# The output projection of a hybrid layer as seven products of half-size blocks instead of eight

## The chip, the cores and the metric

The kernel runs on one core of a Trainium2 chip. The metric is the device time of one execution in microseconds (us), the median of several runs. The engines are named as the profile names them: PE (TensorE, matmuls; PEld are its weight loads), DVE (VectorE), ACT (ScalarE), POOL (GpSimd) and SP (SyncE, which here only issues DMAs).

## What is computed

One layer over 512 tokens of 1024 features: RMSNorm, a combined input projection with 4616 columns, four mLSTM heads and eight heads of block-sparse attention, each with a gate, and one output projection into the residual. All of it is float32. The change touches the end:

```python
def _layer(x, norm_w, w_in, ..., w_out, slopes):
    h = _rmsnorm(x, norm_w)
    proj = h @ w_in
    ...
    y_ml = h_ml.reshape(B, S, ML_WIDTH) * jax.nn.silu(ml_z)      # 512 features
    ...
    y_at = o_at.reshape(B, S, AT_WIDTH) * jax.nn.silu(at_z)      # 512 features
    y = jnp.concatenate([y_ml, y_at], axis=-1) @ w_out           # (512 x 1024) @ (1024 x 1024)
    return x + y
```

## The kernel before

Operands of matmuls are split: a value is kept as a high part in the format fp32r (names ending in hi or h) and the remainder as a low part, fp32r too (lo, l). A product is three matmuls, high by high, high by low and low by high (`mm3`); one of them has 128 x 128 stationary and up to 512 moving columns, and accumulates in a bank of PSUM. A tile is split by two instructions, a cast on ACT that writes the high part and a subtraction on DVE that writes the low one.

The program runs in stages by chunks of w_in's columns: z, aq, ak, av, qk0, qk1, mo, mv and az. Each chunk has 8 k-tiles. Weights come in pieces of two k-tiles, 128 x 1024 elements, 512 KB: SP loads a piece into one of three tiles named raw (`load_w`), ACT casts it to whi, DVE subtracts to wlo (`g_split`); there are six whi and six wlo. az is the last chunk and gives the gate of attention, transposed (features on partitions): `ev_z` multiplies the bank by the tokens' norms on DVE, applies Silu on ACT, multiplies with the attention's result `ot` on DVE, and leaves y_at in cv0 and cv1, four tiles of 128 features by 512 tokens. The mLSTM programs (`g_mlstm`, one for each of four heads) end beside az: PE transposes a head's result into a bank, and `put_y` writes its high part (ACT, with the norm's weight as scale) and its low part (DVE) into two tiles named br. `put_y` does the same for y_at into xh and xl.

The output projection follows. Its k-tiles 0 to 3 are the heads' (br), 4 to 7 attention's (xh, xl). The first half of the output's columns goes tile of 128 tokens by tile, first k 0 to 3 for all four tiles, then k 4 to 7; the second half goes tile after tile with all eight k, and the last tile there is cut into two of 256 columns. All in all that is 4 x 2 x 8 x 3 = 192 matmuls of 512 columns, or their equivalent. Eight pieces of w_out go the way of the weights. x is loaded into tq and tk once they are free; `ev_out` adds a bank and x on DVE, in place, and SP stores the tile.

Everything is one stream per engine, in the order in which the program issues it when it is built. The main stream issues the matmuls; all else are programs (generators) that a planner (`Plan`) resumes between matmuls, when what they wait for is estimated to be there: `Engine` keeps a clock for each engine from costs by element. Nearly all work of DVE, ACT and POOL thus goes through one line of a helper, L75. Matmuls are L173, transposes L177, weight loads L234, loads of x L860, stores L868. On the chip each engine runs its instructions in that order and stops at the first one whose semaphores have not come.

Of the kernel before, what the change touches and what calls it, by code (L numbers as in the profile page):

```python
# [51 lines left out]
class Engine:  # L52
    """Issues to one engine and keeps an estimate of when it gets through."""
# [76 lines left out]

@with_exitstack
def hybrid_layer(ctx: ExitStack, tc: tile.TileContext, xT, x, w_in, w_out, smalls, out):
# [34 lines left out]
    # ---- TensorE  # L167
# [14 lines left out]
    # the table of Silu and the clock of TensorE come up while the first loads run  # L182
# [11 lines left out]
    # ---- weights, in pieces of two k-tiles  # L194
    pieces = []
    off = 0
    for name, cols in _chunks():
        n = len(cols)
        for kk in range(4):
            pieces.append((name, kk, n, w_in, off))  # L200
            off += P * 2 * n
    off = 0
    for half in range(2):
        for kk in range(4):
            pieces.append((f"wo{half}", kk, 512, w_out, off))
            off += P * 2 * 512
# [14 lines left out]
    def load_w(dst=None, between=None):  # L221
        i = nload[0]
        if i >= len(pieces) or (dst is None and i - max(nsplit[0], 5) >= 3):
            return
# [23 lines left out]

    def split_w():
        i = nsplit[0]  # L250
        if i < len(pieces):
            nsplit[0] += 1
            plan.add(g_split(i), rank=1)
# [5 lines left out]
    # ---- constants  # L259
# [12 lines left out]
    # ---- long-lived tiles  # L272
# [19 lines left out]
    xps = Bufs(plan, [sb(f"xp{i}", [P, S + 3]) for i in range(2)])  # L292
    for _, xp in xps.free:
        nc.gpsimd.memset(xp[:, 0:3], 0.0)
# [4 lines left out]
    # ---- startup: x^T and the first weights, into room that is not yet in use  # L299
# [42 lines left out]
    # ---- the three products of the two parts  # L342
# [18 lines left out]

    def group(g, mul, evac):
# [8 lines left out]
    # ---- what follows a projection  # L371
# [53 lines left out]
    # ---- gates of the mLSTM heads  # L425
# [68 lines left out]
    # ---- attention  # L494
# [148 lines left out]
    # ---- mLSTM  # L643
    yh, yl = {}, {}

    def put_y(f, src, scale, t_=0.0):
        hi, lo = (br.get(), br.get()) if f < 4 else (xh[:, f - 4], xl[:, f - 4])
        if scale is None:
            yield act.copy(hi, src)
            t_ = dve.tensor_tensor(lo, src, hi.bitcast(F32), op=ALU.subtract)  # L650
        else:
            yield act.activation(hi, src, AF.Copy, scale=scale)
            t_ = dve.scalar_tensor_tensor(lo, src, scale, hi.bitcast(F32), op0=ALU.mult, op1=ALU.subtract)
        yh[f], yl[f] = hi, lo
        yield t_

    def g_mlstm(h):
# [100 lines left out]
        for t_ in put_y(h, ps, sm[:, C_MN + h:C_MN + h + 1]):  # L758
            yield t_
# [4 lines left out]
    def ev_z(f):  # L764
        z = cv[f // 2][:, f % 2]

        def ev(ps):
# [5 lines left out]
            yield when(lambda: have["proj"], t_)  # L773
            for t_ in put_y(4 + f, z, None):
                yield t_
        return ev

    have["proj"] = 0

    # ---- main stream  # L780
# [62 lines left out]
    plan.until(lambda: have["silu"] == 3)  # L843
    for f in range(4):
        group(f, lambda ps, k: feat_mm(ps, "az", f, k), ev_z(f))
    have["proj"] = 1

    def out_mm(ps, half, t, k, c0=0, c1=512):
        plan.until(lambda: k in yh)
        hi, lo = need_w(f"wo{half}", k // 2)  # L850
        ts = slice(t * P, (t + 1) * P)
        mm3(ps[:, :c1 - c0], yh[k][:, ts], yl[k][:, ts], hi[:, k % 2, c0:c1], lo[:, k % 2, c0:c1],
# [74 lines left out]
```

## Time and profile before

| | us |
|---|---|
| median of 3 runs | 310.79 |
| lowest and highest run | 310.39, 310.81 |
| span of the profiled execution | 308.8 |
| last projection chunk ends, output projection begins on PE | 260.5 |
| last matmul starts | 305.04 |

The profiled execution's own time outside the profiler is not known; its span runs from the first to the last recorded work, and the median of the runs lies 2.0 us above it. In the page, the first part gives each engine's busy time, and the fourth the chain of work that ended last. A window row has the busy time of each engine between two points of the span, then the granted clock of PE as a share of full speed, the share of the DMA engines' time and the rate. A timeline row has the start, the duration from the first instruction's start to the last one's end, the engine, and what it writes from what; "x3" means three alike in a row. Buffer numbers are left out of the names.

### The profile page before, as it was taken

The numbers are of one execution on the slowest core, as the hardware profiler recorded it, in microseconds if no ns is written. First come the engines' busy times: TensorE is split into PE (matmuls) and PEld (weight loads), VectorE is DVE, ScalarE is ACT, GpSimd is POOL, SyncE is SP. The second block draws the span as 40 slices with busy tenths as digits, with TensorE's granted clock in tenths as the row PEclk, the third lists the DMA queues.
The fourth block names the chain that finished last, engine by engine and source line by source line (L and its number), as shares of the span: only waits on it lengthen the run. The fifth ranks groups of instructions, "written<-read, shape, count | busy, mean of one in ns | idle before, by whom it ended". The sixth has DMA issues, their size and how long they took to land.

```text
span 308.8 us, 4284 instructions
## 1 busy us (share of the span) xinstructions
PE 303.2 (98%) x1594; PEld 248.2 (80%) x1594; DVE 185.8 (60%) x395; ACT 150.2 (49%) x271; POOL 58.3 (19%) x94
## 2 busy tenths in 40 slices
PE   7999999999999999999999999999999999999995
PEld 3999888778888868886886888688889978788885
DVE  4892458935456549999627995501568999714111
ACT  3372754314365671775439356899763237420000
POOL 3000164262501800450150005110000060000000
PEclk9999999999999999999999999999999999999999
DMA  7997122141410410132103021400252102832101
GB/s 198 394 412 300 68 69 75 63 137 49 155 70 0 168 39 9 60 128 78 68 2 137 0 83 55 138 0 2 93 176 73 44 24 72 306 135 102 36 34 68
DMA packets 10821, 31.80 MB, mean 103 GB/s; under 512 B 1328, under 2 KB 1584, under 8 KB 10800
## 3 DMA queue, kind: packets, MB, share of 16 engines
q1 hardware_dynamic: 10800, 31.53, 28.8%
q8 instruction: 12, 0.20, 0.3%
q14 instruction: 9, 0.07, 0.1%
HBM read 29.42 MB, written 2.10 MB: 102 GB/s over the span
## 4 chain that ended last, share of the span: by engine, by line
PE 95%; DMA 2%; SPq 1%; DVE 1%; ACT 0%; issue 0%
PE bank L173 89%; PE bank L177 6%; DMA tq<-in_xT_dram 2%; ACT xh L75 0%; DVE wlo L75 0%; SPq L306 0%; DVE xl L75 0%; SPq L234 0%; SPq L232 0%; DVE tk L75 0%; SPq L230 0%; SPq L180 0%
## 5 line engine op out<-in xcount | busy, mean ns | idle before, releaser
L173 PE MATMUL bank<-whi,xh 128*128 128x512 f32 (+2 forms) x260 | 86.4, 367 | 0.7 <-DVE whi L75 0.7
L173 PE MATMUL bank<-wlo,xh 128*128 128x512 f32 (+2 forms) x260 | 85.1, 363 | 0.2 <-DVE wlo L75 0.2
L173 PE MATMUL bank<-whi,xl 128*128 128x512 f32 (+2 forms) x260 | 85.2, 363 | 0.0
L75 DVE TENSOR_TENSOR wlo<-raw,whi 128x1024 fp32r<-128x1024 f32 x39 | 48.0, 1241 | 10.8 <-ACT whi L75 9.2
L173 PEld LDWEIGHTS bank<-whi,xh 128*128 128x128 f32 x260 | 45.1, 188 | 8.7 <-ACT xh L75 1.1
L173 PEld LDWEIGHTS bank<-whi,xl 128*128 128x128 f32 x260 | 45.0, 188 | 8.1
L173 PEld LDWEIGHTS bank<-wlo,xh 128*128 128x128 f32 x260 | 45.1, 188 | 7.9 <-DVE wlo L75 0.6
L75 ACT CAST whi<-raw 128x1024 fp32r<-128x1024 f32 x39 | 40.8, 1048 | 19.8 <-PE bank L173 11.5
L173 PE MATMUL bank<-xh,whi 128*128 128x512 f32 x96 | 40.9, 426 | 0.0
L173 PE MATMUL bank<-xh,wlo 128*128 128x512 f32 x96 | 37.9, 395 | 0.0
L173 PE MATMUL bank<-xl,whi 128*128 128x512 f32 x96 | 37.7, 393 | 0.0
L75 POOL TENSOR_SCALAR b<-b,rec 128x128 f32<-128x128 f32 (+3 forms) x32 | 18.9, 612 | 84.6 <-DVE rec L75 67.1
L75 ACT ACTIVATE br<-bank,sm 64x512 fp32r<-64x512 f32 (+1 forms) x28 | 19.1, 684 | 14.7 <-DVE br L75 9.7
L173 PEld LDWEIGHTS bank<-xh,whi 128*128 128x128 f32 x96 | 18.2, 190 | 4.5 <-issue 2.1
L173 PE MATMUL bank<-whi,br 128*128 128x512 f32 (+1 forms) x72 | 21.4, 370 | 0.0
L173 PEld LDWEIGHTS bank<-xh,wlo 128*128 128x128 f32 x96 | 18.0, 188 | 4.2
L75 ACT ACTIVATE b<-b,mn 128x128 f32<-128x128 f32 (+3 forms) x32 | 17.6, 553 | 7.6 <-DVE mn L75 7.5
L173 PEld LDWEIGHTS bank<-xl,whi 128*128 128x128 f32 x96 | 18.2, 189 | 2.5
L75 DVE SCALAR_TENSOR_TENSOR br<-bank,sm,br 64x512 fp32r<-64x512 f32 (+1 forms) x20 | 15.0, 749 | 5.9 <-ACT br L75 5.6
L75 DVE CUSTOM_DVE_ANT_0 b<-bank,b 128x128 f32<-128x128 f32 (+3 forms) x32 | 14.2, 488 | 5.5 <-PE bank L173 5.4
L173 PEld LDWEIGHTS bank<-whi,br 128*128 128x128 f32 x72 | 13.1, 188 | 2.6
L177 PEld LDWEIGHTS bank<-ident,b 128*128 128x128 f32 (+1 forms) x104 | 12.3, 140 | 3.4 <-issue 0.4
(141 smaller groups left out, 374.1 us busy)
## 6 DMA issues: line engine op xcount, KB each, us to landing
raw<-in_w_in_dram SPq DMA_DIRECT2D x31, 512.0 KB, 3.2
raw<-in_w_out_dram SPq DMA_DIRECT2D x8, 512.0 KB, 3.5
b<-in_w_in_dram SPq DMA_DIRECT2D x3, 520.0 KB, 7.5
tq<-in_xT_dram SPq DMA_DIRECT2D x4, 256.0 KB, 5.4
tk<-in_xT_dram SPq DMA_DIRECT2D x4, 256.0 KB, 7.8
ot<-in_x_dram SPq DMA_DIRECT2D x2, 512.0 KB, 9.1
cv<-in_x_dram SPq DMA_DIRECT2D x2, 512.0 KB, 9.9
tq<-in_x_dram SPq DMA_DIRECT2D x4, 256.0 KB, 5.8
```

The source lines that it names most:

```text
L75: fn(out, *args, **kw)
L173: nc.tensor.matmul(out_, lhsT=lhsT, rhs=rhs, start=start, stop=stop, skip_group_check=True)
L177: nc.tensor.transpose(out_, in_, idn)
```

## The change

With x on the left in halves by tokens (H0, H1) and features (mLSTM, attention) and w_out in four blocks (11, 12, 21, 22), the eight products of blocks become seven, each 256 tokens x 512 features by 512 x 512:

- p5: y_ml of H1 by 11+12; p1: x1 = y_ml H0 - y_at H0, by 11; p2: y_at H0 by 21+11; p6: r = y_ml H1 - x1, by 11-22; p3: c = y_ml H0 - y_ml H1, by 12+22; p7: e = r - y_at H1, by 22; p4: y_at H1 by 21+22. This is also their order on PE.

Each has 4 k-tiles, 2 tiles of 128 tokens and 3 matmuls of 512 columns, 24 in all; the second token tile of p4 is cut into two of 256 columns. Bank pair A accumulates p1, p6, p7 and p4 without a restart, pair B p5 and p3, a third pair p2. What stands in a bank between two products is taken out: after p5, p1 and p6 by a copy on ACT (with scale 1 or -1) into a result tile, to which POOL then issues an accumulating DMA of x from HBM; after p2, p3, p7 and p4 by an addition on DVE into the result tiles. SP stores them.

Sums of weight blocks: 11+12, 21+11, 12+22 and 21+22 are made by a plain load by SP and an accumulating DMA (accum_op add, issued by POOL) of the second block onto it; 11-22 by DVE. Sums of x by DVE, their splits by ACT and DVE. `put_ml` now writes a head's result as float32 to tq on ACT, and splits only H1 at once. The six loads that p5, p1 and p2 need run beside az (`g_load`); the rest of the stage is collected as tasks with costs and set in order by a list scheduler (`Stage`), engine by engine. xp0 and xp1 are one tensor now, since one sum lands there. Lines of the new kernel: matmuls L230, loads L335 and L1041, accumulating loads L339, L1049 (weights) and L1152 (x), casts L1091 and L1110, subtractions L1095, L1105 and L1111, sums for p6 L1085, copies L1151, additions L1141.

```diff
+        if len(AT[tag]) == 2:
+            nc.gpsimd.dma_start(dst, w_src(*AT[tag][1], u), accum_op=ALU.add)
...
-    def put_y(f, src, scale, t_=0.0):
-        hi, lo = (br.get(), br.get()) if f < 4 else (xh[:, f - 4], xl[:, f - 4])
...
-            yield act.activation(hi, src, AF.Copy, scale=scale)
-            t_ = dve.scalar_tensor_tensor(lo, src, scale, hi.bitcast(F32), op0=ALU.mult, op1=ALU.subtract)
...
+    def put_ml(h, ps, scale, t_=0.0):
+        yield act.activation(yml[:, h], ps, AF.Copy, scale=scale)
+        hi, lo = X["p5"]
+        t_ = act.copy(hi(h), yml[:, h, H[1]])
         yield t_
+        yield dve.tensor_tensor(lo(h), yml[:, h, H[1]], hi(h).bitcast(F32), op=ALU.subtract)
...
-    def out_mm(ps, half, t, k, c0=0, c1=512):
...
-    def ev_out(half, t, c0=0, c1=512):
...
+    CHAIN = {"p5": ("B", (1, 1, ADD, False)), "p1": ("A", (0, 0, ADD, False)),
+             "p2": ("1", (0, 0, ADD, True)), "p6": ("A", (0, 1, SUB, False)),
+             "p3": ("B", (0, 1, ADD, True)), "p7": ("A", (1, 1, SUB, True)),
+             "p4": ("A", (1, 0, ADD, True))}
...
+    def load(tag, blk, dst, plus=None, after=()):
+        BT[tag] = dst
+        BL[tag] = st.add("SP", 1450.0, dma(dst, w_src(*blk)), after, lat=2500.0)
+        if plus:
+            BL[tag] = st.add("POOL", 1000.0, lambda: nc.gpsimd.dma_start(dst, w_src(*plus), accum_op=ADD), [BL[tag]], lat=6000.0)
...
+                sums[name, u] = t_ = st.add("DVE", 1240.0, lambda src=src, w2=w2, op=op: nc.vector.tensor_tensor(src, src, w2, op=op), dep)
...
+            dep += (parts(NAMES[n - 3], k=2 * u + 1) if n > 2 else []) + [last]
+            last = st.add("ACT", 1050.0, f_hi, dep)
+            lows[name, u] = t_ = st.add("DVE", 1240.0, f_lo, [last])
...
+        x1.append(st.add("DVE", 420.0, vec(xav[:, f], yml[:, f, H[0]], y_at[f][:, H[0]]), z))
+        xs1.append(split("p1", f, xav[:, f], [x1[f]]))
...
+        if name in ("p5", "p1", "p6"):
+
+            sign = -1.0 if op == SUB else 1.0
+            t_ = st.add("ACT", 640.0, lambda: nc.scalar.activation(d, bank[key, a], AF.Copy, scale=sign), deps)
+            prev[r, c, a, c0] = st.add("POOL", 1000.0, lambda: nc.gpsimd.dma_start(d, x_of(r, c, a), accum_op=ADD), [t_], lat=6000.0)
+            return t_
```

Three places of the order follow. In a row, names carry buffer numbers, and "waits" names the semaphores: Activation, DVE, PE and Pool are engines, DMAHW a DMA that SP issued, DMASW one that POOL issued.

PE at the beginning of the output projection; br are the operands made from mLSTM's results, whi and wlo the weights. Before:

```order
L173 MATMUL bank5_91<-whi_1992,br_0_78 128x512 [waits Activation_49]
L173 MATMUL bank5_91<-wlo_1993,br_0_78 128x512
L173 MATMUL bank5_91<-whi_1992,br_7_85 128x512
L173 MATMUL bank5_91<-whi_1992,br_2_80 128x512 [waits Activation_49]
L173 MATMUL bank5_91<-wlo_1993,br_2_80 128x512
L173 MATMUL bank5_91<-whi_1992,br_3_81 128x512 [waits DVE_49]
```

After, from the same row number:

```order
L230 MATMUL bank1_87<-whi_2062,br_0_78 128x512 [waits Activation_49]
L230 MATMUL bank1_87<-wlo_2063,br_0_78 128x512
L230 MATMUL bank1_87<-whi_2062,br_2_80 128x512 [waits DVE_49]
L230 MATMUL bank4_90<-whi_2062,br_0_78 128x512
L230 MATMUL bank4_90<-wlo_2063,br_0_78 128x512
L230 MATMUL bank4_90<-whi_2062,br_2_80 128x512
L230 MATMUL bank1_87<-whi_2062,br_0_78 128x512 [waits Activation_49]
```

The stage begins at the same place of PE's stream, with two token tiles (two banks) by turns on one weight instead of one token tile after another.

DVE before the projection's first results: the gating of the last head (sz, mst), then lows of br, of weights (wlo) and of x (xl). Before:

```order
L75 SCALAR_TENSOR_TENSOR b5_2_71<-b5_2_71,mst_2213,sz_127 128x128 [waits DVE_49] x2
L75 SCALAR_TENSOR_TENSOR br_3_81<-bank3_89,sm_94,br_2_80 128x512 [waits Activation_49]
L75 TENSOR_TENSOR wlo_2257<-raw_2020,whi_2256 128x1024 [waits DMAHW4_49,PE_49,Activation_49]
L75 TENSOR_TENSOR cv1_132<-cv1_132,ot_133 128x512 [waits Activation_49]
L75 SCALAR_TENSOR_TENSOR br_1_79<-bank2_88,sm_94,br_4_82 128x512 [waits Activation_49]
L75 TENSOR_TENSOR wlo_2280<-raw_2045,whi_2279 128x1024 [waits DMAHW5_49,PE_49,Activation_49]
L75 SCALAR_TENSOR_TENSOR br_5_83<-bank1_87,sm_94,br_6_84 128x512 [waits Activation_49]
L75 TENSOR_TENSOR cv1_132<-bank7_93,rstdb_96 128x512 [waits PE_49]
L75 TENSOR_TENSOR xl_112<-cv0_131,xh_111 128x512 [waits Activation_49]
```

After; b5 holds sums of x, tq the float32 results of mLSTM:

```order
L75 SCALAR_TENSOR_TENSOR b5_2_71<-b5_2_71,mst_2213,sz_127 128x128 [waits DVE_49] x2
L75 TENSOR_TENSOR br_2_80<-tq_128,br_0_78 128x256 [waits Activation_49]
L75 TENSOR_TENSOR cv1_132<-cv1_132,ot_133 128x512 [waits Activation_49]
L75 TENSOR_TENSOR wlo_2258<-raw_1984,whi_2257 128x1024 [waits DMAHW5_49,PE_49]
L75 TENSOR_TENSOR br_2_80<-tq_128,br_0_78 128x256 [waits Activation_49]
L75 TENSOR_TENSOR wlo_2279<-raw_1979,whi_2278 128x1024 [waits DMAHW6_49,PE_49,Activation_49]
L75 TENSOR_TENSOR br_3_81<-tq_128,br_7_85 128x256 [waits Activation_49] x2
L1105 TENSOR_TENSOR b5_3_72<-tq_128,cv0_131 128x256
L1105 TENSOR_TENSOR b5_3_72<-tq_128,cv0_131 128x256 [waits DVE_49]
```

The lows of br are half as wide, and behind them stand sums for the products; 45 instructions stand from here (a row with x2 is two) to the first addition of a result, where before had 14.

ACT in the middle of the stage, before (whi are casts of w_out's pieces, xh those of y_at):

```order
L75 CAST xh_111<-cv0_131 128x512 x2
L75 CAST xh_111<-cv1_132 128x512 [waits DVE_49]
L75 ACTIVATE cv1_132<-cv1_132 128x512 [waits DVE_49]
L75 CAST xh_111<-cv1_132 128x512 [waits DVE_49]
L75 CAST whi_2375<-raw_2145 128x1024 [waits DMAHW6_49,PE_49,Activation_49]
L75 CAST whi_2378<-raw_2277 128x1024 [waits DMAHW7_49,PE_49,Activation_49]
```

After; vbuf and tk hold the two halves of the sum 12+22, sz and vbuf those of 22, b5_4 is r and b5_3 is c, whose casts go to xh and to br_0 and br_7 (p3):

```order
L1091 CAST whi_2416<-raw_1979 128x1024 [waits DVE_49]
L1091 CAST whi_2427<-vbuf_130 128x1024 [waits DMASW4_49,Pool_49]
L1110 CAST xh_111<-b5_4_73 128x512 [waits DVE_49]
L1091 CAST whi_2443<-tk_129 128x1024 [waits DMASW7_49]
L1091 CAST whi_2453<-sz_127 128x1024 [waits DMAHW0_49,PE_49,Activation_49]
L1110 CAST br_0_78<-b5_3_72 128x512 [waits DVE_49]
L1091 CAST whi_2465<-vbuf_130 128x1024 [waits DMAHW2_49,PE_49,Activation_49]
L1110 CAST br_7_85<-b5_3_72 128x512 [waits DVE_49]
```

The cast of c to br_0 stands behind two weight casts, of which the first waits for a DMA that POOL issued.

POOL, before: the last work is a power for mLSTM's norm; no DMA is issued there. After:

```order
L75 TENSOR_TENSOR mst_2213<-mst_2213,mhalf_118 128x4 [waits Pool_49]
L339 DMA raw_1981<-in_w_out_dram 128x1024 [waits DMAHW7_49]
L1049 DMA vbuf_130<-in_w_out_dram 128x1024 [waits DMAHW1_49,PE_49,Activation_49]
L1152 DMA b5_2_71<-in_x_dram 128x512 [waits Activation_49] x2
L1049 DMA tk_129<-in_w_out_dram 128x1024 [waits DMAHW3_49]
L1049 DMA tk_129<-in_w_out_dram 128x1024 [waits DMAHW4_49,DMASW0_49]
L1049 DMA ot_133<-in_w_out_dram 128x1024 [waits DMAHW5_49,DMASW1_49]
L1152 DMA b5_5_74<-in_x_dram 128x512 [waits DMASW2_49,Activation_49]
```

Accumulating loads follow the power; the two of x, behind ACT's copies of p5 to b5_2, stand ahead of the second half of 12+22 in tk.

## Rows read from the trace of the kernel before

**Rows 1.** The page, busy time and chain of the whole span.
```profile
PE 303.2 (98%) x1594; PEld 248.2 (80%) x1594; DVE 185.8 (60%) x395; ACT 150.2 (49%) x271; POOL 58.3 (19%) x94
...
PE 95%; DMA 2%; SPq 1%; DVE 1%; ACT 0%; issue 0%
```

**Rows 2.** Windows: length, busy us of PE, PEld, DVE, ACT, POOL; clock, DMA, GB/s.
```profile
242.00:260.50 18.50, 18.50 (x100) 15.37 (x99) 18.12 (x50) 8.16 (x13) 5.24 (x8) 1.00 0.13 33
260.50:273.00 12.50, 12.50 (x55) 10.01 (x54) 7.63 (x10) 4.55 (x6) 0.00 (x0) 1.00 0.79 289
...
305.40:308.80 3.40, 0.00 (x0) 0.00 (x0) 0.38 (x1) 0.00 (x0) 0.00 (x0) 0.92 0.11 39
```

**Rows 3.** PE's groups by form, 260.5 to 309: count, busy us, mean ns, idle before.
```profile
L173 PE MATMUL bank<-whi,br 128*128 128x512 f32 x56 | 18.3, 396 | 0.0
L173 PE MATMUL bank<-wlo,br 128*128 128x512 f32 x28 | 11.1, 397 | 0.0
L173 PE MATMUL bank<-whi,xh 128*128 128x512 f32 x28 | 11.0, 392 | 0.0
L173 PE MATMUL bank<-whi,xl 128*128 128x512 f32 x28 | 11.0, 392 | 0.0
L173 PE MATMUL bank<-wlo,xh 128*128 128x512 f32 x28 | 11.0, 391 | 0.0
L173 PE MATMUL bank<-whi,br 128*128 128x256 f32 x16 | 3.2, 282 | 0.0
```

**Rows 4.** Timeline, first and last matmuls of the output projection, and the tail.
```profile
260.51 0.39 PE L173 MATMUL bank<-whi,br 128*128 128x512 f32 x1
...
299.48 0.28 PE L173 MATMUL bank<-whi,br 128*128 128x256 f32 x1
...
305.04 0.28 PE L173 MATMUL bank<-whi,xl 128*128 128x256 f32 x1
305.35 0.42 DVE L75 TENSOR_TENSOR tk<-bank,tk 128x256 f32<-128x256 f32 x1 [2.42 <-PE bank L173]
305.81 0.33 SPq L868 DMA_DIRECT2D out_dram<-tk  x1
```

**Rows 5.** Timeline of DVE around the end of az.
```profile
252.72 2.19 DVE L75 SCALAR_TENSOR_TENSOR b<-b,mst,sz 128x128 f32<-128x128 f32 x8
...
255.42 0.75 DVE L75 SCALAR_TENSOR_TENSOR br<-bank,sm,br 128x512 fp32r<-128x512 f32 x1
256.08 1.14 DVE L75 SCALAR_TENSOR_TENSOR b<-b,mst,sz 128x128 f32<-128x128 f32 x4
257.13 0.75 DVE L75 SCALAR_TENSOR_TENSOR br<-bank,sm,br 128x512 fp32r<-128x512 f32 x1
...
262.58 1.89 DVE L75 TENSOR_TENSOR xl<-cv,xh 128x512 fp32r<-128x512 f32 x3
...
266.70 2.36 DVE L75 TENSOR_TENSOR wlo<-raw,whi 128x1024 fp32r<-128x1024 f32 x2 [0.26 <-ACT whi L75]
```

**Rows 6.** DVE's groups by form, 222 to 309.
```profile
L75 DVE TENSOR_TENSOR tk<-bank,tk 128x256 f32<-128x256 f32 x2 | 0.8, 425 | 4.6 <-PE bank L173 4.6
```

**Rows 7.** ACT's groups by form, 222 to 309.
```profile
L75 ACT CAST whi<-raw 128x1024 fp32r<-128x1024 f32 x9 | 9.3, 1046 | 7.6 <-issue 3.0 <-DMA raw<-in_w_in_dram 2.1 <-DMA raw<-in_w_out_dram 2.1
L75 ACT ACTIVATE br<-bank,sm 128x512 fp32r<-128x512 f32 x4 | 2.7, 685 | 3.0 <-PE bank L177 2.9
```

**Rows 8.** DMA issues: count, KB each, median us from issue to landing.
```profile
raw<-in_w_out_dram SPq DMA_DIRECT2D x8, 512.0 KB, 3.5
...
cv<-in_x_dram SPq DMA_DIRECT2D x2, 512.0 KB, 9.9
...
out_dram<-tk SPq DMA_DIRECT2D x2, 128.0 KB, 1.9
```

**Rows 9.** Timelines of SP and POOL: loads of w_out, POOL's last instruction.
```profile
221.62 40.15 SPq L234 DMA_DIRECT2D raw<-in_w_out_dram  x7
...
252.94 1.01 POOL L75 TENSOR_TENSOR mst<-mst,mhalf 128x4 f32<-128x4 f32 x1
```

More of the change, by code (lines that the diff above doesn't have):

```diff
@@ L757, in g_mlstm @@
         yield plan.now + SLACK
-        for t_ in put_y(h, ps, sm[:, C_MN + h:C_MN + h + 1]):
+        yield when(lambda: have["S"] == MLH)
+        if "p5" not in X:
+            X["p5"] = two([br.get() for _ in range(2)]), two([br.get() for _ in range(2)])
+        for t_ in put_ml(h, ps, sm[:, C_MN + h:C_MN + h + 1]):
             yield t_
@@ L890, in hybrid_layer, with ev_keep @@
-    plan.until(lambda: not plan.programs)
+    for j in range(len(LOADS)):
+        plan.add(g_load(j), rank=1)
+    def ev_keep(ps):
+        zlast.append(ps)
+        yield 0.0
+    for f in range(NT):
+        group(f, lambda ps, k: feat_mm(ps, "az", f, k), ev_z(f) if f < 3 else ev_keep)
+    plan.until(lambda: have["y"] == MLH and have["zat"] == 3 and zlast and ("p1", 1) in W and ("p2", 1) in B)
+    st = Stage()
+    ADD, SUB = ALU.add, ALU.subtract
+    xa, xr = b5.get()[:, 0:1024], b5.get()[:, 0:1024]
@@ new lines, in hybrid_layer, with parts, before @@
+    last = None
+    for q in seq:
+        last = PARTS[q] = st.add("PE", 3 * 231.0 * (q[4] - q[3]) / 512, part(*q), [last], lat=0.0)
+    def parts(name, **kw):
+        names = ("name", "a", "k", "c0")
+        return [t for q, t in PARTS.items() if q[0] == name and all(q[names.index(n)] == v for n, v in kw.items())]
+    def before(task, consumers):
+        for c in consumers:
+            c["after"].append(task)
+    rooms = [pair(t[:, 1024 * u:1024 * u + 1024], 512) for t in (flat(sz), vbuf, flat(tk), flat(ot)) for u in range(2)]
@@ new lines, in vec, with split @@
+    def vec(out_, a, b, op=SUB):
+        return lambda: nc.vector.tensor_tensor(out_, a, b, op=op)
+    def split(name, ks, src, dep, war=()):
+        hi, lo = X[name][0](ks), X[name][1](ks)
+        n = 410.0 if isinstance(ks, int) else 650.0
+        h_ = st.add("ACT", n, lambda: nc.scalar.copy(hi, src), [*dep, *war])
+        l_ = st.add("DVE", n + 10, lambda: nc.vector.tensor_tensor(lo, src, hi.bitcast(F32), op=SUB), [h_, *war])
+        for k in ([ks] if isinstance(ks, int) else range(ks.start, ks.stop)):
+            before(l_, parts(name, k=k))
+        return l_
@@ L893 @@
+    sched = st.run({"ACT": max(0.0, act.clock - plan.now), "DVE": max(0.0, dve.clock - plan.now),
+                    "POOL": max(0.0, pool.clock - plan.now)})
 def kernel(x, norm_w, w_in, b_igate, b_fgate, conv_w, conv_b, mlstm_norm_w, q_norm_w, k_norm_w, w_out):
```

302 lines of the change are left out of this document (239 added, 63 removed).

## The prediction, made before the new kernel was run

> **What bounds the kernel now.** The page's first part and its chain of waits come first [rows 1]: TensorE (PE) is busy 303.2 of 308.8 us, 98%, and 95% of the chain that ended last is PE. A kernel like that gets shorter by fewer or shorter matmuls and hardly by anything else. The second view is the table of windows [rows 2]: in the last 18.5 us of the projections, and in the first 12.5 us of the output projection, PE is busy all of the time at granted clock 1.00, the upper of its two levels, 2.4 GHz. VectorE (DVE) is nearly full in the first of these (18.12 of 18.50) and has room in the second (7.63 of 12.50). The last 3.4 us are the tail: no matmul, one eviction, one store.
>
> The third view is PE's groups by form, from the stage's first matmul on [rows 3]: 56+28+28+28+28 = 168 matmuls of 512 columns, and 48 of 256 (16, and four groups of 8 of which one would read like the row shown). PE's timeline gives their pitch [rows 4]: the first starts at 260.51, the first of 256 columns at 299.48, the last at 305.04. So one of 512 costs (299.48-260.51)/168 = 0.232 us, one of 256 costs (305.04-299.48)/47 = 0.118 us. (The mean durations in rows 3, 0.39 and 0.28, overlap and are not the price.)
>
> **What PE saves.** Seven products of 256 tokens by 512 by 512 are 7 x 24 = 168 matmuls of full width where 192 stood. The order of the new kernel has 156 of 512 and 24 of 256 columns. Gone are 12 x 0.232 = 2.78 us and 24 x 0.118 = 2.82 us, together **5.6 us**, every one on the path. In front of the stage nothing moves on PE: its first matmul has the same row number in both orders, and still comes after az, at 260.5. The tail keeps its kind: a matmul of 256 columns, a DVE addition of 128x256, a store of 128 KB [rows 4].
>
> So the products begin at (5.57 us each): p5 260.5, p1 266.1, p2 271.6, p6 277.2, p3 282.8, p7 288.3, p4 293.9, end 299.5. The rest asks who can't hand over in time.
>
> **What DVE adds, and whether it is in time.** From the row behind the last gating of mLSTM on, the new order has 45 preparing instructions on DVE: 14 of 128x1024 (weight lows, two sums for p6), 19 of 512 elements, 12 of 256. Prices are pitches, since neighbours overlap: two of 1024 take 2.36 us and three of 512 take 1.89 [rows 5], so 1.13 and, with the first's start taken off, 0.60 each; for 256 the mean of 425 ns less the same overlap gives 0.33 [rows 6]. Sum 14x1.13 + 19x0.60 + 12x0.33 = 31.2 us, where before had 7.63 us of DVE in the first 12.5 us of the stage [rows 2] and from then on little but results. The start: before ends that gating at 257.1 with one low in front, of 256.08-255.42 = 0.66 [rows 5], that is now gone, so 256.5. If DVE never waits it is through at 287.7. Going down the order, last operand ready against PE's demand: p5 260.7 / 263.8; p1 265.7 / 270.7; p2 first half 266.3 / 271.6, second 269.1 / 274.4; p6 272.6 / 277.2 and 274.9 / 280.0; p3 277.8 / 282.8 and 279.6 / 285.6; p7 282.5 / 288.3 and 284.2 / 289.7; p4 286.0 / 293.9 and 287.7 / 295.3. The least spare is 3 us. Pitches 10% higher would take 3 us off at the end, 0.4 off at p5, and leave more than 2 everywhere.
>
> The results stand behind all that on DVE: the first half of p7 is complete at 291.1 and read by 291.8, before p4 wants its bank at 293.9; the second is read by 294.9, wanted at 296.7. The other result reads have no bank waiting on them. Cost on the path: nothing while the walk holds.
>
> **What ScalarE (ACT) adds.** The weight highs (1.05 each) stay in number per product, and 14 replace 8; six copies out of PSUM are new, priced at the 0.69 of an activation that reads PSUM [rows 7]. In the stage ACT has 10 of the highs, 14 casts of 512 or less at DVE's 0.5 on the mean, and the 6 copies: 10.5 + 7 + 4.1 = 21.6 of 39 us, little over half. It is its order that can hurt, below.
>
> **What the queues add.** The 8 loads of w_out become 12 plain and 8 accumulating ones (6 and 4 of them ahead of the stage), the 8 loads of x become 2 plain and 6 accumulating. The stage's 8 plain ones, 3.7 MB, begin when the first room comes free near 257; at the 289 GB/s of the stage's first window before [rows 2] they are through by 270, and only p6's second sum, at 269, wants one as early as that: the second to be loaded. The early sums for p5 and p2 have the time that SP's row of 221.62 shows [rows 9]: 40 us for seven loads.
>
> The unknown is the **accumulating DMA that POOL issues**; no row shows one. Issue, c: at least SP's 0.33 [rows 4], at most the 1.9 us which a 128 KB store takes altogether [rows 8]; POOL's nearest instruction, the power at 252.94, takes 1.01 [rows 9], and I take 1.0. Landing, L: at least the plain 3.5 of the same size, at most the 9.9 of 16 crowded loads [rows 8]; since it must read its destination too, I take twice the plain, 7. The Trainium skill ("DMA: Bandwidth & Descriptors", section Anatomy of one DMA, SWDGE path) fits 2.0 us plus the bytes over 436e3 for a transfer from this queue, which would be an estimated 3.2 us for 512 KB, and L would be at its lower end; it prices no accumulation, and the sum would not change.
>
> Where it counts: on POOL the second half of p3's weights ("12", u=1) stands behind two loads of x that wait for ACT's copies of p5, the first done at 266.2+0.7, near 267.0. So it lands at 267.0+3c+L. On ACT its high stands three rows ahead of the cast of p3's first x block, with one more weight high between: landing + 1.05 + 0.94 + 0.52, and 0.6 on DVE, must not pass 283.2, where p3 wants its third matmul. So 3c+L may be **13.2 us**; taken 3+7 = 10, spare 3.2. Each us beyond costs PE one. At both upper bounds, 5.7+9.9 = 15.6, PE loses 2.4 us. The halves behind it ("21b", for p4) would land by 267.0+5c+L = 279 and are wanted after 287.
>
> **The sum.** The profiled execution's span is 308.8, and the median 310.79 lies 2.0 above it; the runs spread by 0.4. Span 308.8 - 5.6 = 303.2; I add an allowance of 0.2 for small gaps where seven products change banks and weights; no row shows such a gap. 303.4 + 2.0 = **305.4 us**.
>
> **The rivals.**
> 1. Forecast: the walk holds, 304.9 to 306.3. For it: every spare is 3 us or more, PE is 98% busy with no stall of anybody else's making, and POOL is empty from 254 on. Chance 0.70.
> 2. Partial stalls: DVE goes past its spare (real pitches higher, ACT and DVE waiting on each other by turns, 1 to 3 us), or 3c+L lies between 14.2 and 16.2. For it: DVE is full for 31 us without a gap, and the order of ACT and DVE was laid by estimated costs. Against: before, DVE ran full in 242 to 260.5 and PE still lost nothing [rows 2]. Time 306.4 to 308.4. Chance 0.13.
> 3. Slower: the one accumulating load ("12", u=1) comes so late that ACT, stopped at its high, holds p3's x back and PE stands. Point: 3c+L above 13.2+5.4+0.6 = 19.2, for instance c = 3.1 with L = 9.9, above both bounds that the rows give. At 3c+L = 20 the loss is 6.8: 312.2. Against: the plain loads are over by 270, and POOL has nothing else to do. Chance 0.08.
> 4. POOL cannot issue while DVE runs. The trace has POOL's power of 1.01 us inside eight back-to-back DVE instructions with two inputs from SBUF, as fast as elsewhere [rows 5, 9]; but it has no DMA issue there. If it held for issues, POOL would wait until DVE itself stops for "12", u=0, after its 275.5: four issues and 7 us later, at 286.5, the second half lands, 6.3 us beyond 280.2: 311.7, slower. Chance 0.03. The Trainium skill ("SBUF - State Buffer", the box on the trap of DVE blocking DMA) has this rule for DVE operations in a two-port mode, and under "Who interferes with whom" infers that an addition of two tensors leaves descriptor writing alone; here DVE has only such additions and subtractions in the stage, so by the page nothing is lost, and the trace neither shows nor contradicts it.
> 5. The gain is eaten where the walk doesn't look: POOL had no DMA queue in use before, and what its start and end cost around the span (2.0 us now) could double or triple; or the projections lose to the earlier loads. 307.4 to 311. Chance 0.06, half of it within the bound of no change.
>
> **Chances and range.** A measurement of this kernel can tell some 0.2%, 0.6 us. Faster: cases 1, 2 and half of 5, 0.70+0.13+0.03 = 0.86. Same: half of 5, 0.03. Slower: 3 and 4, 0.11. The range takes in cases 1 and 2, 0.83: from 304.9 (no gaps, and a little for a shorter tail) to 308.4.
>
> **What the profile will show.** Right: PE with 156 matmuls of 512 and 24 of 256 columns behind az, with pitch 0.232, no gap above 0.3 us from 260.5 to 299.5, span near 303.4. DVE full from 256 to 287 with the evictions in a row behind. Accumulating loads that land in 3.5 to 9.9 us, the second half of "12" before 280. Wrong: a gap on PE at p3 near 283 with ACT waiting for a POOL queue (cases 3, 4, which differ in whether POOL's issues are late or their landing is); gaps at other products with DVE as releaser (case 2); a full PE but a time that is more than 2.3 us above the span (case 5); a PE that is slower per matmul, for which nothing in the rows speaks.

## The result and the profile after

The changed kernel takes 306.07 us (median of four runs, 305.93 to 306.64), the kernel before beside it 310.74 (310.39 to 310.81): a ratio of 0.9858, 95% interval 0.9844 to 0.9872, 4.7 us faster. Forecast were 305.4, in a range of 304.9 to 308.4. The profiled execution has a span of 304.2 us.

The page's first part and its chain, then windows (length, busy us of PE, PEld, DVE, ACT and POOL, granted clock, DMA share, GB/s), of the changed kernel:

```profile
PE 299.0 (98%) x1558; PEld 243.2 (80%) x1558; DVE 202.9 (67%) x424; ACT 165.1 (54%) x297; POOL 70.0 (23%) x107
...
PE 97%; DMA 1%; DVE 0%; SPq 0%; issue 0%
```

```profile
260.50:273.00 12.50, 12.50 (x56) 10.21 (x55) 12.50 (x21) 9.66 (x19) 5.37 (x7) 1.00 1.03 325
273.00:286.00 13.00, 13.00 (x58) 10.49 (x57) 11.09 (x16) 10.68 (x16) 3.30 (x4) 1.00 1.01 191
286.00:299.00 13.00, 13.00 (x64) 10.76 (x63) 10.01 (x15) 0.41 (x1) 0.00 (x0) 1.00 0.54 157
```

Against [rows 1] and [rows 2]: PE is still 98% busy and now 97% of the chain. In the stage it has no idle time, while DVE went from 7.63 to 12.50 of the first 12.5 us and ACT from 4.55 to 9.66. In the 13 us behind these the DMA engines are busy throughout (share 1.01) at only 191 GB/s; in the first 12.5 us 325 GB/s go with a share of 1.03. The timeline has the edges, to be read against [rows 4]:

```profile
261.42 0.40 PE L230 MATMUL bank<-whi,br 128*128 128x512 f32 x1
...
283.63 0.39 PE L230 MATMUL bank<-whi,br 128*128 128x512 f32 x1
...
297.57 0.28 PE L230 MATMUL bank<-whi,xh 128*128 128x256 f32 x1
...
300.29 0.28 PE L230 MATMUL bank<-whi,xl 128*128 128x256 f32 x1
300.61 0.42 DVE L1141 TENSOR_TENSOR b<-b,bank 128x256 f32<-128x256 f32 x1 [1.00 <-PE bank L230]
```

From the first output matmul's start to the last one's, the stage takes 300.29-261.42 = 38.87 us, before 305.04-260.51 = 44.53: **5.66 saved**. But the stage begins 0.91 us later than before, and the tail (span's end less the last matmul) is 3.91 instead of 3.76. 5.66-0.91-0.15 = 4.6, the difference of the spans. So the saving is what was forecast, and 0.9 us were lost ahead of the stage, in projections that the change does not touch. The experiments go after three things: where the 0.9 comes from, how much of the 4.7 hangs on the spread work, and what stands next behind PE.

The wait on which the slow rival rested, in the timelines of ACT, DVE and POOL:

```profile
268.59 2.27 POOL L1049 DMA_DIRECT2D tk<-in_w_out_dram  x2
...
278.10 1.05 ACT L1091 CAST whi<-tk 128x1024 fp32r<-128x1024 f32 x1 [2.13 <-DMA tk<-in_w_out_dram]
279.06 1.04 ACT L1091 CAST whi<-sz 128x1024 fp32r<-128x1024 f32 x1
280.00 0.61 ACT L1110 CAST br<-b 128x512 fp32r<-128x512 f32 x1
...
280.65 0.69 DVE L1111 TENSOR_TENSOR br<-b,br 128x512 fp32r<-128x512 f32 x1 [1.62 <-ACT br L1110]
```

ACT does stop at the weight cast of 12+22's second half, for 2.13 us, and DVE behind it for 1.62. The low of p3's first block is done at 281.3, and p3's third matmul comes at 284.1: 2.8 us of spare, where 3.2 were worked out.

### The profile page after: what moved, and what is told of

The parts are those of the page before. It is cut to its first block, busy times and chain, and to the rows that moved or that the text cites. A ratio compares the mean times of both kernels' runs of the same rounds, so it can differ in the third digit from the quotient of the medians.

```text
span 304.2 us, 4297 instructions
## 1 busy us (share of the span) xinstructions
PE 299.0 (98%) x1558; PEld 243.2 (80%) x1558; DVE 202.9 (67%) x424; ACT 165.1 (54%) x297; POOL 70.0 (23%) x107
## 3 DMA queue, kind: packets, MB, share of 16 engines
q0 software_dynamic: 2144, 5.77, 10.5%
## 4 chain that ended last, share of the span: by engine, by line
PE 97%; DMA 1%; DVE 0%; SPq 0%; issue 0%
PE bank L230 91%; PE bank L234 6%; DMA b<-in_w_in_dram 1%; DVE whi L75 0%; DVE b L1141 0%; SPq L413 0%; SPq L237 0%
## 5 line engine op out<-in xcount | busy, mean ns | idle before, releaser
L230 PE MATMUL bank<-whi,xh 128*128 128x512 f32 (+2 forms) x260 | 86.8, 369 | 0.3 <-DVE whi L75 0.3
L230 PE MATMUL bank<-wlo,xh 128*128 128x512 f32 (+2 forms) x260 | 85.7, 365 | 0.0
L230 PE MATMUL bank<-whi,xl 128*128 128x512 f32 (+2 forms) x260 | 85.5, 364 | 0.0
L230 PEld LDWEIGHTS bank<-whi,xh 128*128 128x128 f32 x260 | 45.1, 188 | 9.1 <-ACT xh L75 1.1
L230 PEld LDWEIGHTS bank<-whi,xl 128*128 128x128 f32 x260 | 45.0, 188 | 8.5
L230 PEld LDWEIGHTS bank<-wlo,xh 128*128 128x128 f32 x260 | 45.1, 188 | 8.2 <-DVE wlo L75 0.5
L75 DVE TENSOR_TENSOR wlo<-raw,whi 128x1024 fp32r<-128x1024 f32 x35 | 42.9, 1228 | 11.0 <-ACT whi L75 10.7
L75 ACT CAST whi<-raw 128x1024 fp32r<-128x1024 f32 x35 | 36.7, 1048 | 19.8 <-PE bank L230 11.6
L230 PE MATMUL bank<-xh,whi 128*128 128x512 f32 x96 | 41.0, 427 | 0.0
L230 PE MATMUL bank<-xl,whi 128*128 128x512 f32 x96 | 37.9, 395 | 0.0
L230 PE MATMUL bank<-xh,wlo 128*128 128x512 f32 x96 | 37.8, 394 | 0.0
L75 ACT ACTIVATE br<-bank,sm 64x512 fp32r<-64x512 f32 x24 | 16.4, 684 | 11.7 <-DVE br L75 9.6
L230 PEld LDWEIGHTS bank<-xh,whi 128*128 128x128 f32 x96 | 18.2, 189 | 4.7 <-issue 2.1
L230 PEld LDWEIGHTS bank<-xh,wlo 128*128 128x128 f32 x96 | 18.0, 188 | 4.3
L230 PEld LDWEIGHTS bank<-xl,whi 128*128 128x128 f32 x96 | 18.2, 189 | 2.6
L75 DVE SCALAR_TENSOR_TENSOR br<-bank,sm,br 64x512 fp32r<-64x512 f32 x16 | 12.0, 749 | 5.9 <-ACT br L75 5.7
L230 PE MATMUL bank<-whi,br 128*128 128x512 f32 x48 | 15.3, 392 | 0.0
L75 ACT ACTIVATE b<-bank 128x512 f32<-128x512 f32 x8 | 4.8, 598 | 18.5 <-PE bank L230 18.5
```

What stands on the lines that cost most here:

```text
L75: fn(out, *args, **kw)
L230: nc.tensor.matmul(out_, lhsT=lhsT, rhs=rhs, start=start, stop=stop, skip_group_check=True)
```

## Experiments

**The same two kernels once more.** No edit.

> The changed kernel once more, unedited. Its profile showed the output projection's matmuls taking 38.87 us from the first start to the last, where before took 44.53, a saving of 5.66 as forecast; but its first output matmul came at 261.42, not 260.51, and that 0.91 us is nearly all of what the measured 306.07 has over the forecast 305.4. Theory A: the 0.9 us is how that one profiled execution ran (the lag grows evenly from 13 us on, through stages whose work the change does not touch). Then a second profile puts the first output matmul between 260.2 and 261.5, another place, and the ratio to before may come out near 0.983 to 0.986. Theory B: the change slows the projections (moved tiles, other addresses). Then it stands at 261.4 within 0.15 again while a second profile of before stands at 260.5 within 0.15.

> The kernel before, unedited, for a second profile on the same chip as the run above. Theory A (the lag belongs to the execution): its first output matmul lies closer than 0.4 us to that of the changed kernel's second profile. Theory B (the change slows the projections): 260.5 within 0.15, and the changed kernel 0.7 to 1.1 us later.

Measured: the changed kernel 305.90 us (305.7 to 306.26), ratio 0.9853 (0.9838 to 0.9868); before 310.72 in its one run. The first output matmul stood at 261.22 and 260.76. By the bounds written down neither theory got a clean answer: all starts jitter by some tenths from the first loads on (the first transposes came at 47.01 and 47.25 in the two profiles of the same kernel before). Measured from these transposes instead, which drops that jitter, both answer alike: to the first of the four heads' transposes, near 252 (the expectation of the last run calls it the last head's), it is 204.50 us in both profiles of before (47.01 to 251.51, 47.25 to 251.75) and 205.40 in both of the changed kernel (47.07 to 252.47, 46.88 to 252.28). First and last landmark of the changed kernel:

```profile
47.07 1.05 PE L230 MATMUL bank<-ident,rstd 128*128 128x128 f32 x8
...
252.47 0.60 PE L234 MATMUL bank<-ident,b 128*128 128x128 f32 x4
```

The 0.9 us belongs to the kernel, not to the execution: theory A, the convenient one, falls.

**The late load.** Powers on POOL ahead of the accumulating load of 12+22's second half, two in the first kernel, six in the second:

```diff
-            BL[tag] = st.add("POOL", 1000.0, lambda: nc.gpsimd.dma_start(dst, w_src(*plus), accum_op=ADD), [BL[tag]], lat=6000.0)
+            def late():
+                for _ in range(6 if tag == ("12", 1) else 0):
+                    nc.gpsimd.tensor_tensor(dly, dly, mhalf[:, :4], op=ALU.pow)
+                nc.gpsimd.dma_start(dst, w_src(*plus), accum_op=ADD)
+            BL[tag] = st.add("POOL", 1000.0, late, [BL[tag]], lat=6000.0)
```

> Two powers of 1.02 us each are put on POOL directly ahead of the accumulating load of the second half of 12+22. In the changed kernel that half landed at 278.1, ACT's cast of p3's first x block came at 280.0, its low was done at 281.3, and p3 wanted it with its third matmul at 284.1: spare 2.8 us. Theory (a late landing only uses up spare): 2.04 us later, ACT waits 4.2 instead of 2.1 us at that weight cast, PE never waits, time within 0.3 of the changed kernel, about 306.1. Rival (ACT and DVE have no real spare behind it, since both of their queues stand still meanwhile): PE gaps of 1 to 2 us at p3 or p7, 307 to 308.

> Six powers, 6.1 us, at the same place. Theory, with the landing time of the load unchanged: 12+22's second half lands at 284.2, the low of p3's first x block is done at 287.4, PE waits 3.3 us at p3's third matmul, the time is 309.3. If instead the landing time of 9 us was made by the crowd of other accumulating loads, of which fewer are left by then, the load lands in 5 to 7 us and PE waits 0 to 1.3 us: 306.1 to 307.4. Rival of both (the order is so tight that stalls add up): above 310.

Measured: 305.54 us (305.1 to 305.9), ratio 0.984, with two powers; 311.58 (311.21 to 311.99), ratio 1.0038 (1.0025 to 1.0051), slower than the kernel before, with six. The dose was not as planned: the first power took 5.51 us in both kernels (why is open, see the last section), so POOL was held up for 6.7 and 11.9 us. POOL, ACT and PE with six powers:

```profile
267.32 11.87 POOL L1053 TENSOR_TENSOR dly<-dly,mhalf 128x4 f32<-128x4 f32 x6
279.15 1.80 POOL L1054 DMA_DIRECT2D tk<-in_w_out_dram  x2
...
284.55 1.04 ACT L1097 CAST whi<-tk 128x1024 fp32r<-128x1024 f32 x1 [9.76 <-DMA tk<-in_w_out_dram]
...
287.11 0.79 PE L230 MATMUL bank<-whi,br 128*128 128x512 f32 x1 [4.57 <-ACT br L1116]
287.70 0.63 PE L230 MATMUL bank<-wlo,br 128*128 128x512 f32 x1
```

```profile
279.00:282.50 3.50, 3.50 (x16) 2.54 (x14) 0.00 (x0) 0.00 (x0) 3.50 (x6) 1.00 0.53 70
282.50:287.10 4.60, 0.04 (x1) 0.00 (x0) 0.01 (x1) 2.56 (x4) 1.09 (x2) 0.77 1.05 201
287.10:290.00 2.90, 2.89 (x7) 2.27 (x8) 2.90 (x4) 2.90 (x5) 0.00 (x0) 0.50 1.06 205
```

This is the slow rival made by hand: POOL late, ACT stopped for 9.76 us at one weight cast, p3's first x block behind it, PE idle for 4.57 us. The prediction's rule, landing less 280.2 in its own frame, gives 4.8: this execution's stage began at 260.05, 0.45 ahead of that frame, and 284.55+0.45-280.2 = 4.8. What it lacked is the second price. After the idle stretch PE's granted clock is 0.50, its lower level of 1.2 GHz, and matmuls come every 0.43 us instead of 0.23 until about 291.5. The stage took 305.97-260.05 = 45.92 us, 7.0 more than in the last kernel below, whose weights lie alike; 4.57 are the gap and 2.4 the clock. Here a gap of 4.57 us on PE cost half as much again.

With two powers the half landed at 279.95, in the changed kernel's frame 2.8 later than there, all of its spare. PE shows no gap at p3, but the stage took 39.42 us instead of 38.87: about at the edge. Most of the difference, some 0.4, lies further on, at p4's start at 294.34. (The time is below the changed kernel's 305.90 all the same, since this kernel's projections take 204.55 us; see the last run.) Landing times shrank as the crowd did: in both kernels the delayed load, with fewer others in flight, took 5.4 to 5.5 us from issue to use, where it took 9.5 in the changed kernel.

**Plain instead of accumulating.** All accum_op arguments are taken out.

> All DMAs that POOL issues in the changed kernel (eight of weights, six of x) are made plain: the second block overwrites the first instead of being added, and x overwrites ACT's copies, so these sums are left out; bytes, queue and order stay. In the changed kernel these loads landed in 8 to 14 us for 512 KB while the DMA engines were busy throughout (share 1.01) at only 191 to 211 GB/s, half of what plain loads reach. Theory: the addition doubles the work of the DMA engines and the crowd makes the landing long; then plain ones land in 3.5 to 7 us, the engines' share falls from 1.01 to about 0.6 in 273 to 286, and ACT does not wait at the weight cast of 12+22's second half. The time does not move by more than 0.5 us (305.4 to 306.3), since the late landing was inside the spare. Rival 1: POOL's queue is slow by itself, and landings stay at 8 us or more. Rival 2: the crowd cost PE something, and the time falls by 0.7 us or more.

Measured: 306.11 us (median of two runs). The page's rows of the queue that POOL feeds (packets, MB, share of 16 engines' time), first of the changed kernel, then of this one:

```profile
q0 software_dynamic: 2144, 5.77, 10.5%
```

```profile
q0 software_dynamic: 1632, 5.77, 5.1%
```

The same 5.77 MB cost the DMA engines 10.5% of the span as additions and 5.1% as copies: 181 against 371 GB/s. Loads of 512 KB by POOL from 254 us on (count, KB, median us from issue to landing), again of the changed kernel, then of this one:

```profile
tk<-in_w_out_dram POOLq DMA_DIRECT2D x2, 512.0 KB, 10.5
raw<-in_w_out_dram POOLq DMA_DIRECT2D x1, 512.0 KB, 5.3
...
vbuf<-in_w_out_dram POOLq DMA_DIRECT2D x1, 512.0 KB, 8.4
ot<-in_w_out_dram POOLq DMA_DIRECT2D x1, 512.0 KB, 13.4
```

```profile
tk<-in_w_out_dram POOLq DMA_DIRECT2D x2, 512.0 KB, 5.9
raw<-in_w_out_dram POOLq DMA_DIRECT2D x1, 512.0 KB, 3.7
...
vbuf<-in_w_out_dram POOLq DMA_DIRECT2D x1, 512.0 KB, 6.5
ot<-in_w_out_dram POOLq DMA_DIRECT2D x1, 512.0 KB, 7.1
```

Landings in the stage fell from 8.4 to 13.4 us to 5.6 to 7.1 (raw is the last load ahead of the stage, with little else in flight), ACT did not wait for 12+22's second half, and the time did not move. The issues became cheaper too, 0.53 us each on POOL instead of 0.85. So the additions double the time that these loads take of the DMA engines, and all of that lies inside the spare. Both rivals fall.

**The spread work put back on DVE**, one part at a time and then both:

```diff
-        load(("12", u), (0, 1, u), rooms[3 + u], (1, 1, u))
+        load(("12", u), (0, 1, u), rooms[3 + u])
...
-        load(("21b", u), (1, 0, u), rooms[5 + u], (1, 1, u))
+        load(("21b", u), (1, 0, u), rooms[5 + u])
...
-    SUMS = {"p2": ("p2", None, None), "p6": ("11", "22", SUB), "p3": ("12", None, None), "p7": ("22", None, None),
-            "p4": ("21b", None, None)}
+    SUMS = {"p2": ("p2", None, None), "p6": ("11", "22", SUB), "p3": ("12", "22", ADD), "p7": ("22", None, None),
+            "p4": ("21b", "22", ADD)}
```

> The stage's four accumulating weight loads are undone: 12+22 and 21+22 are made by four DVE additions from the block 22 that lies in SBUF anyway (one early row and the two sums of the first products keep their DMAs). DVE gets 4 x 1.13 = 4.5 us more and one wait of 1.6 us less. Theory (DVE has 3 us and more of room everywhere): last low at 294.1 in the changed kernel's frame, where p4 wants it at 296.6; time as the changed kernel, 305.6 to 306.3. Rival (DVE is already the bound): each us added shows, 308 to 310.

```diff
-        if name in ("p5", "p1", "p6"):
+        if False:
...
-    load_res(1, 0)
+    for rc in ((1, 1), (0, 0), (0, 1), (1, 0)):
+        load_res(*rc)
```

> The other part undone: no copies by ACT and no accumulating loads of x; SP loads x into the result tiles (eight plain loads) and DVE adds the banks of p5, p1 and p6 too, 6 x 0.60 = 3.6 us more. Theory (room of 3 us and more): 305.6 to 306.3, with p6's and p7's first matmuls not waiting for the banks. Rival (a result read stands in DVE's order behind preparations, so that a bank comes free late): a gap of 1 to 3 us at p6 or p7, 306.8 to 309.

> Both parts undone at once: DVE makes the sums 12+22 and 21+22 and adds all results, 8.1 us more; the stage has no DMA issued by POOL. Walked through in the changed kernel's frame with DVE's pitches: first trouble at p7's banks, p6's second result read at 292.5 where its bank is wanted at 292.0; then p4's operands, 0.1 to 0.4 late; PE loses about 1.0 us, and the last additions queue up for some 0.3 more. Theory: 307.1 (306.3 to 308). Rival A (room is larger than walked): 305.6 to 306.2. Rival B (DVE is far over, or PE's clock falls with gaps): above 308.5.

Measured: sums on DVE 306.36 us, ratio 0.9865 (0.985 to 0.988), not told apart from the changed kernel; results on DVE 306.69, 0.9876 (0.9861 to 0.989), 0.8 above its 305.90; both 307.41, 0.9897 (0.9881 to 0.9914), 1.5 above. The sums alone came out at the upper edge of what was worked out (306.3), both together close to it (307.1). The results alone came out between theory and rival, and neither had the cause: no bank came free late, but p3's second x block and p7's operands came a few tenths late, because four of the eight plain loads of x went ahead of 12+22's second half in SP's order and POOL then waited 6.5 us for that load. PE and the bank reads on DVE with both parts undone:

```profile
292.71 0.50 PE L230 MATMUL bank<-whi,xh 128*128 128x512 f32 x1 [0.41 <-DVE b L1142]
...
297.79 4.65 DVE L1142 TENSOR_TENSOR b<-b,bank 128x512 f32<-128x512 f32 x9
```

The only recorded gap stands where the walk put it, at p7's second bank, and nine additions queue up at the end. So accumulating DMAs and ACT's copies together are worth about 1.5 us of the change; the other part of the gain is there without them.

**Less and more work on PE.** First, two matmuls per product instead of three (the cross terms are left out); then an eighth product's matmuls put back, into a bank that nobody reads:

```diff
-            mm3(bank[key, a][:, c0:c1], xs[0](k)[:, ts], xs[1](k)[:, ts], hi[:, k % 2, c0:c1], lo[:, k % 2, c0:c1],
+            ps_, x_ = bank[key, a][:, c0:c1], xs[0](k)[:, ts]
+            mm(ps_, x_, hi[:, k % 2, c0:c1], k == 0 and (name in ("p5", "p1", "p2") or key == "1"), False)
+            mm(ps_, xs[1](k)[:, ts], lo[:, k % 2, c0:c1], False, k == 3)
```

> Of the three matmuls of each product only two stay in the stage (high by high and low by low, so that every operand is still waited for; the two cross terms are left out): 56 matmuls of 512 columns fewer on PE, 13.0 us. DVE, ACT and POOL keep all their work and order. Theory (behind PE stands DVE, through with its last low near 291 in any case, with p7's bank reads behind it on DVE): p4 starts near 292.3, ends near 296.1, and the time falls by about 4 us only, to 302 (301.5 to 303.5; more if PE's granted clock falls in the gaps). Rival (PE alone matters): the whole 13 us, 293.

```diff
+            if name == "p2":
+                mm3(extra, xs[0](k)[:, ts], xs[1](k)[:, ts], hi[:, k % 2, c0:c1], lo[:, k % 2, c0:c1], True, True)
```

> The changed kernel with an eighth product's worth of matmuls put back: p2's 24 matmuls of 512 columns are done once more into a bank that nobody reads. Nothing else changes. Theory (the change is worth exactly its matmuls): 24 x 0.2317 = 5.56 us more than the changed kernel, 311.5 (311.0 to 311.9), that is 0.8 above the kernel before: the allowance for a longer start, tail and small gaps. Rival (part of the gain came from elsewhere, results begun early by ACT or a better order): under 310.5, at or below the kernel before.

Measured: 303.12 us (302.68 to 303.56) with 13.0 us of matmuls gone, and 311.48 (311.26 to 311.78), ratio 1.0032 (1.002 to 1.0043), with 5.56 put back. The second says that the gain is that of the matmuls; what the change costs beside them (0.9 ahead of the stage, 0.15 in the tail) is why this kernel is even slower than before. The first says how far that can go. Its gaps on PE and who ended them:

```profile
280.36 0.60 PE L230 MATMUL bank<-whi,br 128*128 128x512 f32 x1 [2.47 <-ACT br L1111]
...
292.17 0.50 PE L230 MATMUL bank<-whi,xh 128*128 128x512 f32 x1 [1.86 <-DVE b L1142]
...
294.89 0.38 PE L230 MATMUL bank<-whi,xh 128*128 128x256 f32 x1 [0.59 <-DVE b L1142]
```

p4 began at 292.17, within 0.2 of the walk, since p7's banks are read by DVE behind all its preparations. But the longest gap, at p3, is not DVE's, as the theory had it: ACT had stood 2.93 us for the landing of 12+22's second half, and PE behind it. The clock fell there too:

```profile
280.40:283.00 2.60, 2.47 (x6) 1.67 (x7) 2.60 (x4) 2.60 (x4) 0.00 (x0) 0.54 1.06 202
```

Of 13 us only about 3 came through.

**DVE held up.** Six idle additions stand ahead of the first sum of x:

```diff
+    for _ in range(6):
+        nc.vector.tensor_tensor(rooms[0], rooms[0], rooms[0], op=ADD)
```

> Six idle DVE additions of 128x1024, 6.8 us, stand ahead of the first sum of x. In the changed kernel p1's first low was done at 264.2 where p1's third matmul wants it at 267.4, a spare of 3.2. Theory (a spare of about 3 us, then each us costs PE one): PE waits 3.5 us at p1's third matmul, the products behind it gain spare by the same 3.5, nothing else waits; 309.5, and up to 2.5 more if the gap lets PE's clock fall as the gap of 4.57 us at p3 did. Rival A (other engines' waits absorb it): 306 to 307. Rival B (DVE is the bound throughout, all 6.8 show): 312.8 without a clock loss.

Measured: 311.51 us (311.33 to 312.45), ratio 1.0035.

```profile
261.89 7.52 DVE L1177 TENSOR_TENSOR sz<-sz 128x1024 f32<-128x1024 f32 x6
...
270.24 0.50 PE L230 MATMUL bank<-whi,br 128*128 128x512 f32 x1 [3.05 <-ACT br L1110]
...
271.40 1.22 PE L230 MATMUL bank<-whi,br 128*128 128x512 f32 x2 [0.44 <-DVE br L1111]
```

```profile
267.00:271.00 4.00, 0.91 (x3) 0.30 (x2) 3.96 (x7) 1.02 (x3) 0.00 (x0) 1.00 1.02 249
271.00:275.00 4.00, 3.60 (x10) 2.89 (x11) 4.00 (x10) 4.00 (x9) 0.28 (x1) 0.57 0.32 68
```

PE waits 3.05 and 0.44, together the 3.5 forecast, then runs at the lower clock for some 3 us (0.57 from 271 to 275), and nothing later waits. The six took 7.4 us instead of 6.8 (261.89 to 269.33). p1's third matmul came at 271.40, where 24 pitches and two more behind 261.50 give 267.5: 3.9 late, so the spare was 3.5, a little more than the 3.2 expected. Of the 5.6 lost, 3.5 are the gaps; the rest goes with the lower clock.

**The place of the tiles behind xp.** The merged tensor xp is shorter than the two tiles it replaces: 4128 bytes on a partition instead of 4160. All that is laid out behind it (raw, whi, wlo, small tiles) therefore lies 32 bytes lower than before. Worked out from the tiles' sizes, each rounded up to 32 bytes, whi begins on multiples of 64 bytes, in the kernel before 32 past them; no profile shows an address. The two late kernels, which have a small extra tile ahead of xp, were the only variants with the old places, and the only ones with 204.5 us in the projections. The last kernel keeps every instruction and its order:

```diff
-    xpt = sb("xp", [P, 2, S + 4])
+    xpt = sb("xp", [P, 2, S + 8])
```

> The changed kernel with the tensor xp (the two former tiles xp0 and xp1 in one) 32 bytes longer on each partition: 4160 bytes, as much as the two tiles took before. Every instruction and its order are the same; raw, whi and wlo, which are laid out behind xp, return to the addresses they have in the kernel before, 32 bytes up. From the first transposes at 47 us to those of the last head near 252, ten profiles of the changed kernel and its variants with whi 32 bytes lower take 205.40 us; two of the kernel before, and the two late-load variants (whose extra small tile moved everything up by 32 bytes), take 204.50 to 204.55. Theory (the place of the weights costs PE these 0.9 us): 204.5 here, the first output matmul about 0.9 earlier against the first transposes than in the changed kernel, time 305.0 (304.6 to 305.4), about 0.9 below the changed kernel's and nearer the forecast. Rival (the extra tile itself, or POOL's work, did it in the late variants): 205.4 and 305.9. The output stage itself, 38.87 us from its first matmul to its last, may move by 0.2 either way with the same addresses.

Measured: **304.97 us** (304.71 to 305.26), ratio 0.9827 (0.9813 to 0.9841): faster than the changed kernel by 0.9 (0.8 by the ratios) and the fastest of all that compute the whole layer. Chains of waits: two steps with equal matmuls (start, us, count), of the changed kernel, of before, and of this one:

```profile
65.67 19.76 PE bank L230 x84
...
166.13 25.73 PE bank L230 x119
```

```profile
65.45 19.60 PE bank L173 x84
...
165.58 25.51 PE bank L173 x119
```

```profile
65.25 19.60 PE bank L230 x84
...
165.38 25.51 PE bank L230 x119
```

PE's steps are 0.8% longer with the tiles 32 bytes lower, with no wait in either, and equal to before's to the hundredth with the tiles back. From the first transposes to the first head's it is 204.49 us (46.81 to 251.30), against 205.40 in the changed kernel and its variants with the low places (nine profiles, not ten as the expectation has it):

```profile
46.81 1.05 PE L230 MATMUL bank<-ident,rstd 128*128 128x128 f32 x8
...
251.30 0.60 PE L234 MATMUL bank<-ident,b 128*128 128x128 f32 x4
```

The shape of xp itself is not the cause: the late kernels keep it, and have 204.55. Which of the moved tiles matters was not separated; of them PE reads whi and wlo, but that these are the ones is not shown. In the output stage the effect is not there: 38.96 us from first to last matmul against 38.87.

## Why the prediction was right, and where it was not

*The matmuls* (5.6): right. Measured 5.66 in the stage; putting 24 back added 5.6, where their pitch gives 5.56. (24 x 0.118 is 2.83 and not 2.82, which changes nothing.)

*"In front of the stage nothing moves on PE ... its first matmul still comes after az, at 260.5"*: this step failed, and it is nearly all of the distance between 305.4 and 306.07. The order of instructions did not move; their operands' addresses did. The diff's line on xp was read as a change of storage and priced at nothing. Case 5 did name a loss in the projections, but with the earlier loads as its cause; the run with the old places has these loads too and loses nothing. The last sign of being wrong, a PE that is slower per matmul, is the one that came, in the projections. With the places restored the time is 304.97, and the forecast would have been 0.4 too high: the allowance of 0.2 for gaps was not needed, since no product begins with one.

*DVE's walk*: prices right, places close. The last low was done at 291.2, walked to 287.7; of the 3.5 between them 0.9 is the later stage, 1.6 DVE's wait behind ACT, which the walk left out though it named ACT's stop, and about 1 us small waits and a later start. PE never noticed. For p1 the walk lists the last operand alone, with 5.0 us of spare. p1's first one has less: of 7.4 us of idle additions 3.9 reached PE there, so its spare was 3.5. The least spare of 3 us stands all the same.

*The accumulating DMA*: c was taken as 1.0 and measured 0.85 to 1.09 where it stood alone (up to 2.1 in a row of three); L was taken as 7 and measured 8.4 to 13.4 for 512 KB. L was reckoned for one transfer and not for the crowd: the last one ahead of the stage, with little else in flight, landed in 5.3 us, below 7, and in the stage a load shares the DMA engines with others that also cost double. The landing came at 278.1; forecast 277.0, 277.9 with the later stage. The spare left was 2.8, forecast 3.2. The reason to trust the conclusion was that both upper ends, a sum of 15.6, cost PE only 2.4. Single values passed these ends (13.4 against 9.9), but for the load that counts 3c+L was 10.7 (267.36 to 278.10), inside.

*The slow rival* was sound in mechanism and place: made late by hand, the load stops ACT, DVE and then PE, us for us. Its price was too low, as a gap of that size also lowers PE's clock, another 2.4 us.

*POOL shut out by DVE*: was not seen for DMA issues. DVE was busy in all of 12.50 us [window 260.50:273.00 above], and POOL's issues there took 0.86 us for one and 1.73 for two, up to 2.27 for two in the longer row; with DVE idle two took 1.80 [279.15 in the kernel with six powers]. The inference that the Trainium skill's page "SBUF - State Buffer" draws under "Who interferes with whom", that such additions leave descriptor writing alone, agrees with these rows.

*Partial stalls* did not occur in the changed kernel; the kernel with both parts on DVE shows how near they are: 8.1 us more of DVE cost 1.5.

## What to carry to other kernels

Where one engine is busy 98% of the time, count its instructions at their pitch and then spend the effort on who must hand over in time: a walk down the other engines' orders with pitches from the trace gave spares here that held within half a us at the two places where they were tried, p1 and p3; at the walk's end the waits that it leaves out came to 2.6 us. A tile that changes size moves all tiles behind it: compare their addresses, not only the order, and measure an untouched stage from one landmark to another to see it. A late operand can cost more than its lateness: behind PE's gaps of 3.05 and 4.57 us here the clock was at its lower level for some us.

## What was not expected of the hardware

- With the tiles behind xp 32 bytes lower (raw, whi, wlo, small tiles), matmuls of the projections take 0.4% longer over all (205.40 against 204.50 us), single steps up to 0.9%, though no wait is recorded. The output stage, on the same whi and wlo, shows nothing of it (38.87 against 38.96).
- Accumulating DMAs from HBM into SBUF cost the DMA engines twice the time of copies of the same bytes, 10.5% against 5.1% of the span for 5.77 MB, and POOL 0.85 us an issue instead of 0.53.
- A power of 128x4 on POOL took 5.51 us while DVE ran additions of two SBUF operands without a gap, and 1.01 to 1.03 us in the kernel before; the five that followed took 1.0 to 1.5. DMA issues by POOL in the same stretch were not slowed. The page "SBUF - State Buffer" of the Trainium skill, section "Who interferes with whom", has this exclusion for a POOL operation that reads SBUF; that DVE was the cause is not shown by a run of its own. Against it stands that the five ran beside DVE instructions of the same kind, and that the slow one was the first behind two DMA issues of POOL's.
- PE's granted clock behind its gaps: 0.50 for 4.4 us of matmuls after 4.57 us without work, 0.50 for 3 us after 3.05 and 0.44, 0.54 for 2.6 us after 2.47 in the kernel with two matmuls per product. After the gap of 1.86 in that kernel it stayed at 1.00.
